# Windowed attention of a two-layer encoder: the two halves of its output added by a transfer, and part of the normalising and rounding done on GpSimd

## The chip, the cores and the metric

The kernel runs on one core of a Trainium2 chip. The core has a matrix engine (TensorE, PE in the profile), VectorE (DVE), ScalarE (ACT), GpSimd (POOL) and SyncE (SP), which only issues transfers, and 16 DMA engines. Each engine works through its own instructions in order. The metric is the device time of one execution in microseconds (us); the median over several runs is compared.

## The reference, cut to what matters

Two layers over a sequence of 1024 tokens with 1024 features. The first layer's mixer is windowed attention; the change lies in it and in the start of its output projection.

```python
def mixer_window_attn(u, mem_kv, w_in, sink, w_out, pos):
    q, k, v, xq = jnp.split(u @ w_in, [...], axis=-1)    # 16 query heads, 4 key/value heads of 64
    q = rope(q, pos); k = rope(k, pos)
    o = window_gqa_sink(q, k, v, sink)
    return jnp.concatenate([o, memory_cross_attn(xq, mem_kv)], axis=-1) @ w_out

# window_gqa_sink, per block of 128 queries, over up to 3 blocks of 128 keys:
    s = q k^T / 8, masked to |qpos - kpos| <= 128
    m = max(max_k s, sink);  p = exp(s - m)
    p = p / (sum_k p + exp(sink - m))
    o = p v
# memory_cross_attn: 4 heads of 128 over 256 memory rows, softmax, no mask
```

After the mixer come a norm, a gated feed-forward layer, and a second layer with another mixer (a gated linear recurrence). Everything is float32.

## The kernel before

Every product is made of single-pass float32r matmuls on operands that are split in two: `h` is the value rounded to float32r, `l` the remainder (`split`, line 87: ACT casts `h`, DVE subtracts to get `l`); `mm3` runs three matmuls (h·h, h·l, l·h). TensorE has therefore about three times the plain work and is the engine that all others feed.

`window()` goes through four groups `g`, one for each key/value head and its four query heads `j`. `proj(g)` makes queries, keys and values of 8 blocks of 128 tokens (`pj` banks), rotates them (DVE: two multiplications into `t1`, `t2`; POOL: the two additions into `rq`, lines 298 and 299), and TensorE turns them (`ptq`). `attend(g)` then works on 8 row blocks `n`. For each:

- scores of the four heads (`ps`, lines 374 and 375), evicted by DVE with mask and sink (line 377, `sm`), `exp` by ACT with its sum (line 381);
- the reciprocal of the sums (DVE, line 386) and the four heads' scaling by it: heads 0 and 1 on ACT (line 389), heads 2 and 3 on DVE (line 391);
- for each of up to three key blocks: four transposes of `sm` (`pt`, line 396), the split into `ph` and `pl` (lines 88 and 89), and two matmuls with `v` that add up in the bank `po` (lines 399 and 400). The stationary `v` holds the rounded part in columns 0 to 63 and the remainder in columns 64 to 127, so the rows 64 to 127 of `po` must be added to rows 0 to 63;
- that addition: ACT copies the upper rows to the tile `o` (line 402), DVE adds the lower rows (line 403).

After every second block the pair's `o` (two buffers) is sent off by SP, in two transfers: for groups 0 to 2 to the array `oT[0]` in device memory (line 414), for group 3 straight into the remainder array `ul` (line 408), where `split_moved` (lines 350 to 353) then splits it in place into `uh` and `ul`, ACT first and DVE after it.

Between the blocks of `attend` run units of cross attention (`cross_unit`; its division by the sums is line 231, one DVE instruction for four row blocks) and the projection of the next group. In group 3 there is no next group: the output projection `wo0` takes that place. `Out.begin` reads `oT[0]` back for eight token blocks (`Out.read`, ACT cast in line 466, DVE subtraction in line 467) and multiplies them by the part of the weights that belongs to the first 6 of 12 feature blocks. `Out.finish` adds the cross heads (`Out.cross`, tiles `oh`, `ol`) and the feature blocks 6 and 7, which are group 3's and come from `split_moved`.

What stands in a row on each engine is set when the program is built: the tile scheduler simulates the engines and takes instructions by priority as they become ready. `tc.issue_after(x)` keeps an instruction behind `x`. Transfers issued by SP go through a hardware queue, those issued by POOL through a software queue; only POOL's can add to what is at the target. POOL's queue also carries 24 large transfers in `window()` that add up second-layer-of-feed-forward weights (`w2s`, lines 144 and 146).

Of the kernel before, what the change touches and what calls it, by code (L numbers as in the profile page):

```python
# [8 lines left out]
F32 = mybir.dt.float32  # L9
# [4 lines left out]
ALU = mybir.AluOpType  # L14
# [35 lines left out]
def build(tc, A, out):  # L50
# [149 lines left out]
    def cross_unit(l, h, b, head, wp, tags, w0, pair, dead=False):  # L200

        wh, wl, kvh, kvl = head
        ps = tags["pj"][2].tile([P, 512], F32, tag=tags["pj"][0], bufs=tags["pj"][1], name="pj")
        for k in range(KT):
            c = slice(k * P, (k + 1) * P)
            m = slice(b * 512, (b + 1) * 512)
            mm3(ps, wh[:, c], wl[:, c], uh[:, k, m], ul[:, k, m], k == 0, k == KT - 1)
        xh, xl = pair("x", b)
        with tc.high_priority(AHEAD):
            if l == 0:  # L210
                split(xh, xl, ps)
            else:
                act.activation(xh, ps, AF.Copy, scale=XSCALE)
                dve.scalar_tensor_tensor(xl, ps, XSCALE, xh.bitcast(F32), op0=ALU.mult, op1=ALU.subtract)
        p = wp.tile([P, 4, 385 if l == 0 else 256], F32, tag="sm", bufs=tags["sm"], name="xp")[:, :, :256]
        st = {x: wp.tile([P, 4], F32, tag=x, name=x) for x in ("nm", "su", "rd")}
        for i in range(2):
            s = tags["ps"][2].tile([P, 2, 256], F32, tag=tags["ps"][0], bufs=tags["ps"][1], name="ps")
            for j in range(2):
                m = slice((2 * i + j) * P, (2 * i + j + 1) * P)  # L220
                mm3(s[:, j, :], xh[:, m], xl[:, m], kvh[:, 0, :], kvl[:, 0, :], True, True)
            e = slice(2 * i, 2 * i + 2)
            dve.reduce_max(st["nm"][:, e], s, axis=AX.X, negate=True)
            if l == 0:
                dve.tensor_tensor(st["nm"][:, e], st["nm"][:, e], xsc[:, 4 * b + 2 * i:4 * b + 2 * i + 2], op=ALU.mult)
            for j in range(2):
                q = 2 * i + j
                act.activation(p[:, q, :], s[:, j, :], AF.Exp, bias=st["nm"][:, q:q + 1],
                               scale=xsc[:, 4 * b + q:4 * b + q + 1] if l == 0 else 1.0, accum_out=st["su"][:, q:q + 1])
        dve.reciprocal(st["rd"], st["su"])  # L230
        dve.tensor_tensor(p, p, bc(st["rd"].unsqueeze(2), [P, 4, 256]), op=ALU.mult)
        po = tags["po"][b]()
        for m in range(2):
            tp = tags["pt"][2].tile([P, 4, P], F32, tag=tags["pt"][0], bufs=tags["pt"][1], name="pt")
            for q in range(4):
                pe.transpose(tp[:, q, :], p[:, q, m * P:(m + 1) * P], ident)
            ph, pl = pair("p", m)
            split(ph, pl, tp.rearrange("p a b -> p (a b)"))
            hd = slice(m * P, (m + 1) * P)
            mm3(po, kvh[:, 1, hd], kvl[:, 1, hd], ph, pl, m == 0, m == 1)  # L240
        ot = p[:, :2, :].rearrange("p a b -> p (a b)") if dead else w0.tile([P, 512], F32, tag=tags.get("xo", "xo"), bufs=1, name="xo")
        act.copy(ot, po)
        act.dma_start(oT[l][8 + h, :, b * 512:(b + 1) * 512], ot)


    def window():
# [5 lines left out]
            ap_.tile([P, 4], F32, tag=x, name=x)  # L252
        wmask = ap_.tile([P, 384], F32, bufs=1, name="wmask")
        sk = ap_.tile([P, 16], F32, bufs=1, name="sk")
        ap_.tile([64, 4, 256], F32, tag="o", bufs=2, name="o")
        for x, n in (("kh", 1), ("kl", 1), ("v", 1), ("qs", 8), ("ph", 2), ("pl", 2)):
            if x == "v":
                ap_.tile([P, NT, P], F32R, tag=x, bufs=n, name=x)
# [87 lines left out]

        marks, moved = {}, []

        def split_moved():
            ts_ = moved.pop()  # L350
            oh, ol = uh[:, 6:8, ts_], ul[:, 6:8, ts_]
            act.copy(oh, ol.bitcast(F32))
            dve.tensor_tensor(ol, ol.bitcast(F32), oh.bitcast(F32), op=ALU.subtract)

        def attend(g, qkv, blocks=range(NT)):
            qs, kh, kl, v = qkv
            for b in range(2):
                for nn in range(4):
# [1 line left out]
                    if n not in blocks:  # L360
                        continue
                    if nn % 2 == 0:
                        pairs[0] = ap_.tile([64, 4, 256], F32, tag="o", bufs=2, name="o")
                    o = pairs[0]
                    lo, hi = max(n - 1, 0), min(n + 2, NT)
                    w = (hi - lo) * P
# [13 lines left out]
                    for j in range(4):  # L380
                        marks[g, n] = act.activation(sm[:, j, :w + 1], sm[:, j, :w + 1], AF.Exp, bias=st["nm"][:, j:j + 1],
                                                     scale=-1.0, accum_out=st["su"][:, j:j + 1])
                    if moved and n % 2 == 0:
                        with tc.issue_after(marks[g, n].ins):
                            split_moved()
                    dve.reciprocal(st["rd"], st["su"])
                    for j in range(4):
                        if j < 2:
                            act.activation(sm[:, j, :w], sm[:, j, :w], AF.Copy, scale=st["rd"][:, j:j + 1])
                        else:  # L390
                            dve.tensor_scalar_mul(sm[:, j, :w], sm[:, j, :w], st["rd"][:, j:j + 1])
                    po = psp.tile([P, 4, P], F32, tag="po", bufs=1, name="po")
                    for c in range(hi - lo):
                        tp = psp.tile([P, 4, P], F32, tag="pt", bufs=2, name="pt")
# [4 lines left out]
                        pe.matmul(po, v[:, lo + c, :], ph, start=c == 0, stop=False)  # L399
                        pe.matmul(po, v[:, lo + c, :], pl, start=False, stop=c == hi - lo - 1)  # L400
                    ov = o[:, :, (nn % 2) * P:(nn % 2 + 1) * P]
                    act.copy(ov, po[64:])
                    dve.tensor_tensor(ov, po[:64], ov, op=ALU.add)
                    if nn % 2 == 1 and g == 3:
                        ts_ = slice((n - 1) * P, (n + 1) * P)
                        moved.append(ts_)
                        for hp in range(2):
                            nc.sync.dma_start(ul[hp * 64:(hp + 1) * 64, 6:8, ts_].bitcast(F32), o[:, hp::2, :])
                        if n == NT - 1:
                            split_moved()  # L410
                    elif nn % 2 == 1:
                        ts_ = slice((n - 1) * P, (n + 1) * P)
                        for hp in range(2):
                            nc.sync.dma_start(
                                oT[0][2 * g:2 * g + 2, hp * 64:(hp + 1) * 64, ts_].rearrange("a d t -> d a t"),
                                o[:, hp::2, :])
                if 4 * b + 3 not in blocks:
                    continue
                for _ in range(XU[g][b]):
# [12 lines left out]
        attend(3, cur)  # L432
        wo0.open()
        y0 = wo0.w1.tile([P, NT, 512], F32, bufs=1, name="y0")
        wo0.begin(psq, ("pj", "pj", "ptq"), [y0[:, t, :] for t in range(NT)], {6: marks[3, 2], 7: marks[3, 2]})
        psp.release()
        ap_.release()
        x0.release()
# [2 lines left out]
    class Out:  # L441
# [19 lines left out]
        def read(self, ks, c0, c1, eng, behind=None):  # L461
            c = (slice(None), slice(ks[0], ks[-1] + 1), slice(c0, c1))
            raw = ul[c].bitcast(F32)
            eng.dma_start(raw, oT[self.l][ks[0]:ks[-1] + 1, :, c0:c1].rearrange("k p t -> p k t"))
            with tc.issue_after(behind.ins) if behind else nullcontext():
                act.copy(uh[c], raw)
            dve.tensor_tensor(ul[c], raw, uh[c].bitcast(F32), op=ALU.subtract)

        def kept(self, ps, t, ks, first, last):
# [1113 lines left out]
```

## Time and profile before

| | us |
|---|---|
| median of 3 runs | 2645.28 |
| lowest, highest | 2643.67, 2646.74 |
| the profiled execution's own time | 2646.48 |
| its span, first to last instruction | 2644.4 |
| TensorE busy in the span | 2598.7 (98%) |
| DVE, ACT, POOL busy in the span | 1807.8, 1379.0, 486.7 |

`window()` takes the stretch from about 60 us to 493 us after the span's start; from 400 us on, the output projection runs between its last blocks. The profile gives a page for the whole span, and answers questions on a stretch of it: busy time of each engine by stretch, groups of equal instructions with their mean duration and what ended the idle time before them, waits by engine with what released them, and the instructions in order of time. A row such as `L403 DVE TENSOR_TENSOR o<-po,o 64x512 ... x28 | 19.0, 677` reads: line 403, on DVE, writes `o` from `po` and `o`, 64 partitions by 512 elements, 28 times, 19.0 us in all, 677 ns each.

### The profile page before, as it was taken

Reading aid. Unit: us, or ns where it says so; the run is one execution under the profiler, and the core shown is the slowest. Engines: PE = TensorE matmul, PEld = TensorE weight load, DVE = VectorE, ACT = ScalarE, POOL = GpSimd, SP = SyncE. Lnnn points to the kernel's source line nnn. Section 1 sums busy time; section 2 is a strip of 40 time slices with the busy share of each in tenths; the row PEclk is TensorE's granted clock in tenths of the full one; section 3 lists DMA queues with packets and bytes.
Section 4 is the critical chain, followed back from the end, with each engine's and each line's share of the span. In section 5 each row is a group of like instructions: output and inputs, shape, how many; then the busy total and the mean of one; then the engine's idle time right before and its main releaser. Section 6 shows DMA issues by size and latency. Waiting matters only on the chain. (4 is left out here: it accounts for less than half of the span.)

```text
span 2644.4 us, 38978 instructions
## 1 busy us (share of the span) xinstructions
PE 2598.7 (98%) x14420; PEld 2187.7 (83%) x14420; DVE 1807.8 (68%) x2875; ACT 1379.0 (52%) x2471; POOL 486.7 (18%) x552
## 2 busy tenths in 40 slices
PE   8999999999999999999999999999999999999998
PEld 8988887887888888887888888888887788888887
DVE  6778777587656565488688686887757665656447
ACT  6667767445444444455465554555534444444443
POOL 0421120221111100032234131231311111110013
PEclk9999999999999999999999999999999999999999
DMA  9782232367877757673236351103337777785666
GB/s 354 248 191 46 74 102 69 126 190 187 210 200 197 198 158 251 201 258 127 85 112 162 85 119 47 54 32 116 121 113 191 197 196 203 202 206 166 219 193 236
DMA packets 195726, 425.92 MB, mean 161 GB/s; under 512 B 20048, under 2 KB 56272, under 8 KB 189904
## 3 DMA queue, kind: packets, MB, share of 16 engines
q1 hardware_dynamic: 161552, 324.06, 38.0%
q0 software_dynamic: 24544, 90.19, 16.5%
q10 hardware_dynamic: 9440, 9.19, 1.0%
q8 instruction: 113, 1.85, 0.3%
q14 instruction: 77, 0.63, 0.1%
HBM read 330.04 MB, written 116.39 MB: 169 GB/s over the span
## 5 line engine op out<-in xcount | busy, mean ns | idle before, releaser
L89 DVE TENSOR_TENSOR wl<-st,wh 128x1024 fp32r<-128x1024 f32 (+1 forms) x238 | 262.8, 1111 | 318.0 <-ACT wh L88 291.5
L88 ACT CAST wh<-st 128x1024 fp32r<-128x1024 f32 (+1 forms) x238 | 222.1, 935 | 286.1 <-PE X L588 186.4
L83 PE MATMUL pj<-uh,wh 128*128 128x512 f32 x512 | 202.5, 396 | 3.4 <-DVE q L1139 2.0
L588 PE MATMUL X<-wl,wh 128*128 128x512 f32 x528 | 204.7, 389 | 0.3 <-DVE wl L89 0.3
L588 PE MATMUL X<-wh,wl 128*128 128x512 f32 x528 | 204.5, 389 | 0.0
L85 PE MATMUL pj<-uh,wl 128*128 128x512 f32 x512 | 202.3, 395 | 0.0
L84 PE MATMUL pj<-ul,wh 128*128 128x512 f32 x512 | 200.9, 392 | 0.1
L588 PE MATMUL X<-wh 128*128 128x512 f32 x528 | 198.7, 390 | 0.3 <-ACT c L1002 0.3
L83 PE MATMUL pj<-wh,uh 128*128 128x384 f32 (+1 forms) x512 | 189.5, 371 | 3.7 <-DVE gs L1125 2.4
L84 PE MATMUL pj<-wl,uh 128*128 128x384 f32 (+1 forms) x512 | 187.2, 366 | 0.0
L85 PE MATMUL pj<-wh,ul 128*128 128x384 f32 (+1 forms) x512 | 187.2, 366 | 0.0
L79 DVE TENSOR_TENSOR wl<-st,wh 128x1024 fp32r<-128x1024 f32 (+1 forms) x91 | 118.3, 1305 | 33.9 <-ACT wh L78 33.3
L588 PE MATMUL V<-uh,wh 128*128 128x512 f32 x336 | 130.7, 389 | 0.0
L588 PE MATMUL V<-ul,wh 128*128 128x512 f32 x336 | 130.7, 389 | 0.0
L588 PE MATMUL V<-uh,wl 128*128 128x512 f32 x336 | 130.7, 389 | 0.0
L78 ACT CAST wh<-st 128x1024 fp32r<-128x1024 f32 (+1 forms) x97 | 97.6, 1012 | 40.9 <-PE pj L84 26.9
L588 PEld LDWEIGHTS X<-wh 128*128 128x128 f32 x528 | 99.1, 188 | 21.7 <-ACT c L1002 0.7
L588 PEld LDWEIGHTS X<-wl,wh 128*128 128x128 f32 x528 | 99.1, 188 | 20.9 <-DVE wl L89 0.8
L588 PEld LDWEIGHTS X<-wh,wl 128*128 128x128 f32 x528 | 99.1, 188 | 20.7
L83 PEld LDWEIGHTS pj<-uh,wh 128*128 128x128 f32 x512 | 96.3, 188 | 22.8 <-DVE q L1139 2.9
L971 POOL TENSOR_TENSOR c<-c,g 128x512 f32<-128x512 f32 x24 | 42.6, 1793 | 388.3 <-PE X L588 160.1
L84 PEld LDWEIGHTS pj<-ul,wh 128*128 128x128 f32 x512 | 96.2, 188 | 19.2 <-DVE ul L89 0.4
(410 smaller groups left out, 7217.6 us busy)
## 6 DMA issues: line engine op xcount, KB each, us to landing
st<-hid SPq DMA_DIRECT2D x154, 256.0 KB, 3.1
st<-in_ffw_dram SPq DMA_DIRECT2D x108, 256.0 KB, 3.2
w2s<-in_ffw_dram POOLq DMA_DIRECT2D x24, 1024.0 KB, 8.5
st<-in_ffw_dram SPq DMA_DIRECT2D x46, 512.0 KB, 4.3
hid<-tt SPq DMA_DIRECT2D x88, 256.0 KB, 4.8
st<-w2s SPq DMA_DIRECT2D x88, 256.0 KB, 3.0
sx<-in_ffw_dram SPq DMA_DIRECT2D x84, 256.0 KB, 4.0
sy<-in_ffw_dram SPq DMA_DIRECT2D x42, 512.0 KB, 6.8
```

The costliest lines, as they stand in the source:

```text
L78: act.copy(h[:, :n], raw)
L79: (eng or dve).tensor_tensor(l[:, :n], raw, h[:, :n].bitcast(F32), op=ALU.subtract)
L83: pe.matmul(o, ah, bh, start=first, stop=False)
L84: pe.matmul(o, ah, bl, start=False, stop=False)
L85: return pe.matmul(o, al, bh, start=False, stop=last)
L88: act.copy(h, src)
L89: dve.tensor_tensor(l, src, h.bitcast(F32), op=ALU.subtract)
L588: last = pe.matmul(o, x, y, start=new, stop=e, skip_group_check=not first)
L971: pool.tensor_tensor(y[q][:, t, :], y[q][:, t, :], g3[:, c], op=ALU.mult)
```

## The change

1. The addition of the two halves leaves DVE. `o` gets 128 partitions, ACT copies all of `po` into it. SP sends the upper half to the target (groups 0 to 2 now in one transfer instead of two), and an adding transfer on POOL's queue (`add_parts`, line 358) puts the lower half on top. The adding transfers of a pair are issued behind the scaling of the next block that follows the pair; those of the last pair at once. `split_moved` moves from the even block after a pair to the odd one.
2. Of the four heads' scaling, head 0 stays on ACT, head 1 goes from ACT to DVE, heads 2 and 3 go from DVE to POOL.
3. In the first layer's cross units, DVE divides two of the four row blocks in one instruction, POOL the other two in two.
4. In the first layer's `Out.read`, the cast of the rows that are read back goes from ACT to POOL, and token blocks 6 and 7 no longer wait for a mark in group 3.

```diff
@@ cross_unit
         dve.reciprocal(st["rd"], st["su"])
-        dve.tensor_tensor(p, p, bc(st["rd"].unsqueeze(2), [P, 4, 256]), op=ALU.mult)
+        n = 2 if l == 0 else 4
+        dve.tensor_tensor(p[:, :n], p[:, :n], bc(st["rd"][:, :n].unsqueeze(2), [P, n, 256]), op=ALU.mult)
+        for q in range(n, 4):
+            pool.tensor_scalar_mul(p[:, q, :], p[:, q, :], st["rd"][:, q:q + 1])
@@ window
+        summed = []
+
+        def add_parts(behind=None):
+            while summed:
+                dst, src = summed.pop(0)
+                with tc.issue_after(behind.ins) if behind else nullcontext():
+                    pool.dma_start(dst, src, accum_op=ALU.add)
+
         def split_moved():
-            ts_ = moved.pop()
+            ts_ = moved.pop(0)
@@ attend
-                        pairs[0] = ap_.tile([64, 4, 256], F32, tag="o", bufs=2, name="o")
+                        pairs[0] = ap_.tile([P, 4, 256], F32, tag="o", bufs=2, name="o")
...
-                    if moved and n % 2 == 0:
+                    if moved and n % 2 == 1:
                         with tc.issue_after(marks[g, n].ins):
                             split_moved()
                     dve.reciprocal(st["rd"], st["su"])
                     for j in range(4):
-                        if j < 2:
+                        if j == 0:
                             act.activation(sm[:, j, :w], sm[:, j, :w], AF.Copy, scale=st["rd"][:, j:j + 1])
+                        elif j == 1:
+                            dve.tensor_scalar_mul(sm[:, j, :w], sm[:, j, :w], st["rd"][:, j:j + 1])
                         else:
-                            dve.tensor_scalar_mul(sm[:, j, :w], sm[:, j, :w], st["rd"][:, j:j + 1])
+                            scaled = pool.tensor_scalar_mul(sm[:, j, :w], sm[:, j, :w], st["rd"][:, j:j + 1])
+                    add_parts(scaled)
...
-                    act.copy(ov, po[64:])
-                    dve.tensor_tensor(ov, po[:64], ov, op=ALU.add)
-                    if nn % 2 == 1 and g == 3:
+                    act.copy(ov, po)
+                    if nn % 2 == 1:
                         ts_ = slice((n - 1) * P, (n + 1) * P)
-                        moved.append(ts_)
-                        for hp in range(2):
-                            nc.sync.dma_start(ul[hp * 64:(hp + 1) * 64, 6:8, ts_].bitcast(F32), o[:, hp::2, :])
+                        if g == 3:
+                            moved.append(ts_)
+                            parts = [(ul[hp * 64:(hp + 1) * 64, 6:8, ts_].bitcast(F32), slice(hp, 4, 2)) for hp in range(2)]
+                        else:
+                            rows = oT[0].rearrange("k p t -> (k p) t")[256 * g:256 * g + 256, ts_]
+                            parts = [(rows.rearrange("(j d) t -> d j t", d=64), slice(4))]
+                        for dst, js in parts:
+                            nc.sync.dma_start(dst, o[64:, js, :])
+                            summed.append((dst, o[:64, js, :]))
                         if n == NT - 1:
-                            split_moved()
-                    elif nn % 2 == 1:
...
+                            add_parts()
+                            while moved:
+                                split_moved()
...
-        wo0.begin(psq, ("pj", "pj", "ptq"), [y0[:, t, :] for t in range(NT)], {6: marks[3, 2], 7: marks[3, 2]})
+        wo0.begin(psq, ("pj", "pj", "ptq"), [y0[:, t, :] for t in range(NT)], {})
@@ Out.read
             with tc.issue_after(behind.ins) if behind else nullcontext():
-                act.copy(uh[c], raw)
+                if self.l:
+                    act.copy(uh[c], raw)
+                else:
+                    pool.tensor_copy(uh[c], raw)
```

Since the scheduler orders the program anew, the rows on every engine move. Three places matter for what follows.

POOL, in the middle of group 1. `L298`/`L299` (after the change `L301`/`L302`) are the rope additions, `L370` (`L381`) puts the sink beside the scores, `L144` is a large weight transfer. Before:

```order
L370 COPY sm<-sk 128x4
L298 TENSOR_TENSOR rq<-t_2925,t_2926 128x320
L299 TENSOR_TENSOR rq<-t_2925,t_2926 128x64
L144 DMA w2s_79<-w2s_79 32x3x2048
L370 COPY sm<-sk 128x4 x2
L298 TENSOR_TENSOR rq<-t_2960,t_2961 128x320
L299 TENSOR_TENSOR rq<-t_2960,t_2961 128x64
```

and with the change, where `L404` is the scaling of heads 2 and 3 and `L358` the adding transfer of a pair:

```order
L381 COPY sm<-sk 128x4
L404 TENSOR_SCALAR sm<-sm,rd 128x384 x4
L358 DMA oT_57<-o 64x4x256
L301 TENSOR_TENSOR rq<-t_2917,t_2918 128x320
L302 TENSOR_TENSOR rq<-t_2917,t_2918 128x64
L144 DMA w2s_79<-w2s_79 32x3x2048
L404 TENSOR_SCALAR sm<-sm,rd 128x384 x2
L381 COPY sm<-sk 128x4 x2
L301 TENSOR_TENSOR rq<-t_2952,t_2953 128x320
L302 TENSOR_TENSOR rq<-t_2952,t_2953 128x64
```

The rope additions, which waited for nothing but DVE's two multiplications, now stand behind scalings that wait for a softmax, and behind a transfer that waits for SP's.

ACT, at the end of group 3, from the copy of block 5 to the last split. `o<-po` is the copy, `uh<-ul` the split of a pair in place (lines 352, 363), `ph<-pt` the cast of a key block's transposes. Before:

```order
L402 COPY o<-po 64x4x128
L88 CAST ph<-pt 128x512
L352 CAST uh<-ul 128x2x256
L88 CAST ph<-pt 128x512 x2
L402 COPY o<-po 64x4x128
L88 CAST ph<-pt 128x512
L402 COPY o<-po 64x4x128
L352 CAST uh<-ul 128x2x256
```

with the change:

```order
L416 COPY o<-po 128x4x128
L88 CAST ph<-pt 128x512 x2
L363 CAST uh<-ul 128x2x256
L88 CAST ph<-pt 128x512
L416 COPY o<-po 128x4x128
L88 CAST ph<-pt 128x512
L416 COPY o<-po 128x4x128
L363 CAST uh<-ul 128x2x256
```

The split of pair 4-5 (the first `uh<-ul` in both) still stands two to three rows behind the copy of block 5, and the cast for block 6's third key block now stands directly behind it.

TensorE, the same place: block 6's matmuls with `v` and its neighbours. `pb<-xwh,uh` is the first product that reads the feature blocks 6 and 7 of pair 4-5. Before:

```order
L399 MATMUL po<-ph,v 128x512
L400 MATMUL po<-pl,v 128x512
L399 MATMUL po<-ph,v 128x512
L400 MATMUL po<-pl,v 128x512
L396 MATMUL pt<-ident,sm 128x128 x4
L83 MATMUL pb<-xwh,uh 128x512
L84 MATMUL pb<-xwl,uh 128x512
```

with the change:

```order
L413 MATMUL po<-ph,v 128x512
L414 MATMUL po<-pl,v 128x512
L413 MATMUL po<-ph,v 128x512
L414 MATMUL po<-pl,v 128x512
L410 MATMUL pt<-ident,sm 128x128 x4
L413 MATMUL po<-ph,v 128x512
L414 MATMUL po<-pl,v 128x512
L410 MATMUL pt<-ident,sm 128x128 x4
L83 MATMUL pb<-xwh,uh 128x512
L84 MATMUL pb<-xwl,uh 128x512
```

The third pair of `po` matmuls of block 6, which stood 11 rows behind the first product on `uh`, now stands ahead of it. From block 5's last `po` matmul up to this point TensorE has, in both programs, that matmul, eight transposes, 16 products `pb<-..,uh` of other tokens, four `po` matmuls and four transposes.

More of the change, by code (lines that the diff above doesn't have):

```diff
@@ L254, in window @@
         sk = ap_.tile([P, 16], F32, bufs=1, name="sk")
-        ap_.tile([64, 4, 256], F32, tag="o", bufs=2, name="o")
+        ap_.tile([P, 4, 256], F32, tag="o", bufs=2, name="o")
         for x, n in (("kh", 1), ("kl", 1), ("v", 1), ("qs", 8), ("ph", 2), ("pl", 2)):
@@ L401, in attend @@
                     ov = o[:, :, (nn % 2) * P:(nn % 2 + 1) * P]
-                    act.copy(ov, po[64:])
-                    dve.tensor_tensor(ov, po[:64], ov, op=ALU.add)
-                    if nn % 2 == 1 and g == 3:
+                    act.copy(ov, po)
+                    if nn % 2 == 1:
                         ts_ = slice((n - 1) * P, (n + 1) * P)
-                        moved.append(ts_)
-                        for hp in range(2):
-                            nc.sync.dma_start(ul[hp * 64:(hp + 1) * 64, 6:8, ts_].bitcast(F32), o[:, hp::2, :])
-                        if n == NT - 1:
-                            split_moved()
-                    elif nn % 2 == 1:
[L412 to L416, printed above, removed]
+                        if g == 3:
[7 more added lines that the diff above has]
+                            summed.append((dst, o[:64, js, :]))
+                        if n == NT - 1:
+                            add_parts()
+                            while moved:
+                                split_moved()
                 if 4 * b + 3 not in blocks:
```

## The prediction

> **What bounds the kernel now.** I read the page's busy shares, then busy time by stretch, then TensorE's waits in the stretches the change touches, then the groups of instructions it edits, and last the order of time at the end of group 3.
>
> ```profile
> span 2644.4 us, 38978 instructions
> PE 2598.7 (98%) x14420; PEld 2187.7 (83%) x14420; DVE 1807.8 (68%) x2875; ACT 1379.0 (52%) x2471; POOL 486.7 (18%) x552
> ```
>
> TensorE is busy 98% of the span and sets the time. No matmul is added or removed, so the change can only move TensorE's idle time and its clock. Busy time by stretch (us, counts, granted clock, share of the DMA engines):
>
> ```profile
> 60.00:150.00 90.00, 86.78 (x499) 79.75 (x497) 66.10 (x181) 55.36 (x132) 34.98 (x59) 1.00 0.78 236
> 150.00:240.00 90.00, 87.88 (x504) 79.00 (x503) 68.26 (x169) 63.46 (x156) 21.22 (x33) 0.98 0.59 134
> 240.00:345.00 105.00, 101.05 (x578) 88.53 (x578) 83.07 (x198) 77.09 (x189) 15.86 (x24) 1.00 0.21 61
> 345.00:398.00 53.00, 49.74 (x287) 45.41 (x286) 38.90 (x79) 32.30 (x72) 11.97 (x15) 0.97 0.35 105
> 398.00:458.00 60.00, 57.57 (x288) 46.85 (x287) 44.38 (x105) 47.06 (x106) 1.01 (x5) 1.00 0.24 71
> 458.00:520.00 62.00, 62.00 (x293) 51.55 (x292) 32.88 (x47) 25.46 (x54) 15.03 (x9) 1.00 0.34 107
> ```
>
> The first five rows hold 398 us, of which TensorE is busy 383.02: 15.0 us are idle. The granted clock falls to 0.98 and 0.97 in two of them, which stands for 90 x 0.02 + 53 x 0.03 = 3.4 us of full-speed work, some 1.7 in each. The last row, where the end of group 3 runs beside the output projection, has no idle at all. So at most 15.0 + 3.4 = 18.4 us can be gained, and between 458 and 520 us one can only lose. TensorE's waits from 60 to 458 us (us in total, times, longest):
>
> ```profile
> PE po L399 <- ACT ph L88: 2.8, 4, 1.1
> PE ptq L321 <- DVE kl L89: 1.9, 1, 1.9
> PE po L400 <- DVE pl L89: 1.5, 2, 1.0
> PE pt L396 <- ACT sm L389: 1.4, 2, 0.7
> PE ps L374 <- DVE nm L377: 1.3, 4, 0.4
> ...
> PE ptq L321 <- POOL rq L299: 0.9, 1, 0.9
> PE ptq L321 <- POOL rq L298: 0.8, 2, 0.5
> PE pb L83 <- ACT y L500: 0.8, 1, 0.8
> PE po L399 <- ACT xo L242: 0.7, 1, 0.7
> PE pt L396 <- DVE pl L89: 0.7, 1, 0.7
> ```
>
> They are short and spread over many producers on DVE and ACT; no one chain dominates.
>
> **The change part by part.** The edited groups from 60 to 458 us, with busy us and mean ns (the MEMSET from the whole span):
>
> ```profile
> L391 DVE TENSOR_SCALAR sm<-sm,rd 128x384 f32<-128x384 f32 x48 | 19.2, 442 | 0.4
> L403 DVE TENSOR_TENSOR o<-po,o 64x512 f32<-64x512 f32 x28 | 19.0, 677 | 7.3 <-ACT o L402 7.3
> L231 DVE TENSOR_TENSOR xp<-xp,rd 128x1024 f32<-128x1024 f32 x8 | 10.0, 1254 | 0.3
> L389 ACT ACTIVATE sm<-sm,rd 128x384 f32<-128x384 f32 x48 | 27.2, 611 | 2.3 <-DVE rd L386 2.2
> L466 ACT CAST uh<-ul 128x768 fp32r<-128x768 f32 x8 | 6.6, 835 | 4.0 <-DMA ul<-oT 4.0
> L298 POOL TENSOR_TENSOR rq<-t,t 128x320 f32<-128x320 f32 x32 | 29.0, 905 | 133.8 <-DVE t L297 75.6 <-DVE xss L1389 24.4 <-DVE rd L230 12.4
> L79 POOL TENSOR_TENSOR wl<-st,wh 128x768 fp32r<-128x768 f32 x6 | 11.2, 1880 | 2.4 <-ACT wh L78 2.4
> L1094 POOL MEMSET Az<- 128x512 f32 x2 | 1.0, 528 | 0.0
> ```
>
> *DVE and ACT get lighter.* Per block DVE drops one of two scalings (0.44) and the addition (0.68): 1.12 us; ACT drops one scaling, 0.61. Block work shortens a wait only where the late producer stands behind it, by no more than the wait's length. I take each wait down by what its engine saves: the four on `ph` by 0.61 each, 2.4 together; the one on `kl` by 1.1; the two on `pl` (line 400) whole, 1.5; the four on `nm` whole, 1.3; `y` 0.6; `xo` 0.6; `pl` (line 396) 0.7. That is -8.2 us. If stalls of this sort are what brings the clock down, one of the two drops goes: -1.7. The rest of the 15 us idle has no recorded releaser; I take nothing from it. Between nothing and the 15.0 + 3.4 lies -9.9.
>
> *Scaling on POOL.* No row shows POOL scaling by a column. Below stands the memset, 528 x 384/512 = 0.40 us for 384 elements; above, half of line 79 (two operands, twice the width), 0.94. I take the middle, 0.67, since the scaling reads one full operand, the memset none and line 79 two. A block's pair takes 1.34. POOL and DVE can also keep each other out:
>
> ```profile
> 92.79 3.65 POOL L79 TENSOR_TENSOR wl<-st,wh 128x768 fp32r<-128x768 f32 x2
> 92.95 3.90 DVE L391 TENSOR_SCALAR sm<-sm,rd 128x256 f32<-128x256 f32 x2
> ```
>
> Two DVE scalings took 3.90 us for well under 0.9 while POOL ran. The trace therefore shows one of the two held up until the other engine is done; in a block DVE now scales (0.44) at the same moment as POOL, so POOL's pair ends after up to 1.34 + 0.44 = 1.78, where ACT's pair ended after 2 x 0.61 = 1.22. The two waits of `pt` on ACT's scaling become waits on POOL's, 0.56 longer each: +1.1. The Trainium skill, page "GPSIMD Engine Reference", section "1. Specifications", says that GpSimd shares its SBUF interface with VectorE, which speaks against giving the two engines work at one moment; by it, every block would pay in one order or the other; the row above agrees, with 3.90 us.
>
> *The rope additions* now stand on POOL behind scalings. The three recorded waits on `rq` (1.7 us) each grow by up to one scaling, 0.67: +2.0. Behind the same scalings stand the adding transfers and the large weight transfers of lines 144 and 146; the first of these are read after group 2's attention, the second in the second layer, so their 0.6 to 1.1 us of issue is costed at nothing. With 85 of 398 us POOL was idle enough; its new work is 28 pairs x 1.34 + 8 reads + divisions + 12 issues, about 77 us, 41% in all.
>
> *Taken at nothing.* The read casts: 8 x 0.835 leave ACT and come to POOL at 0.79 to 1.88 (the same two bounds); no wait of TensorE is on `uh` from line 466. The cross division: DVE's 1254 halves, POOL takes two scalings of 256; the wait on `xo` lies behind it and is counted. ACT's copy keeps 512 elements per partition on twice the partitions. SP issues 12 transfers fewer in groups 0 to 2. `o` has two buffers and is free only when the adding transfer has read it; the order leaves over a block (398/28 = 14 us) for that. The cover for all of these is other blocks' and units' products in TensorE's order; without it, a late `o` would hold ACT's copy and the `ph` cast behind it.
>
> *End of group 3.* Here something new enters a chain that TensorE waits on. Before, for pair 4-5 (start, us busy):
>
> ```profile
> 477.00 0.39 PE L400 MATMUL po<-pl,v 128*128 128x512 f32 x1
> 477.43 0.58 ACT L402 COPY o<-po 64x512 f32<-64x512 f32 x1
> 478.05 0.68 DVE L403 TENSOR_TENSOR o<-po,o 64x512 f32<-64x512 f32 x1
> 478.76 1.25 SPq L408 DMA_DIRECT2D ul<-o  x2
> 481.86 0.62 ACT L352 CAST uh<-ul 128x512 fp32r<-128x512 f32 x1 [3.23 <-DMA ul<-o]
> 483.01 0.47 PE L83 MATMUL pb<-xwh,uh 128*128 128x512 f32 x1
> ```
>
> The cast waited 3.23 us for the transfer and began 4.9 us after the last `po` matmul; TensorE got to its first product on `uh` 6.0 us after that matmul, in time. With the change the chain drops the addition (0.7), so the upper half is in place at 4.9 - 0.7 = 4.2 us; then POOL issues the adding transfer. Rows for that, median us from issue to landing in the last column:
>
> ```profile
> ul<-o SPq DMA_DIRECT2D x8, 128.0 KB, 2.4
> sy<-sx POOLq DMA_DIRECT2D x42, 256.0 KB, 4.2
> ```
>
> `sy<-sx` is the same kind, an adding transfer between tiles, with twice the bytes; the plain `ul<-o` has the right size. I take 4.2 as the nearer kind and 2.4 as the lower bound; the second half's issue runs beside the first half's flight. The cast starts at 8.4, ends at 9.0. The cast of block 6's third key block (0.58, as the copy) now stands directly behind it, so `ph` comes at about 9.6, plus some 0.3 us of handing over between five engines (an estimate; the gaps in the rows are 0.03 to 0.04, a transfer's end is not among them): 9.9. TensorE has between the two `po` matmuls the same instructions as it had before its first product on `uh`, so it waits 9.9 - 6.0 = 3.9 us (2.1 with the lower bound), and one clock drop of 1.7 with it: +5.6. Pair 2-3 has more room, at most 0.7, left to the range; of pair 6-7 the order leaves 48 products ahead of the use, 48 x 62/293 = 10.2 us, against the 9.0 of the cast's end: nothing.
>
> The page "DMA: Bandwidth & Descriptors" of the Trainium skill, section "Anatomy of one DMA — SWDGE (gpsimd) path", fits a transfer from that queue as a fixed 2.0 us plus its bytes at 436 GB/s: an estimate of 2.3 us for 128 KB, by which the stall would be 2.0 instead of 3.9. For 256 KB the same fit gives 2.6 where the row above has 4.2, so this trace does not bear the fit out for adding transfers.
>
> *Sum.* -9.9 + 1.1 + 2.0 + 5.6 = -1.2 us against the profiled execution, 2646.5: 2645.3. That execution is 1.2 above the median of the runs, so against the median the forecast is 2644.1.
>
> **The rivals.** A measurement of this kernel tells about 0.2% (5.3 us) from no change.
>
> *The end costs nothing.* If the adding transfer lands as soon as a plain one and the casts stay ahead of TensorE, only -9.9 + 3.1 = -6.8 is left: 2638.5. For it: the lower bound takes away 1.8 of the 3.9. Against: the chain is serial, 4.2 us before the transfer even begins, and TensorE has 6.0.
>
> *GpSimd becomes the late one (slower).* One mechanism: the scaling takes the upper bound, 0.94, and is held up by DVE. Then a pair takes 2 x 0.94 + 0.44 = 2.3 us against ACT's 1.22, +1.1 at every place where scaled scores come just in time. Waits on scores and casts make 9 to 12 such places, +10 to +13, with the clock drops of two of them (3.4): about +13 in place of the 1.1 and 2.0. -9.9 + 5.6 + 13 = +9: 2654. It decides from about 1 us per scaling. For it: line 79's 1880 and the 3.90 above. Against: the transposes come many products after the scaling in TensorE's order.
>
> *The waits don't go.* If the waits come from the order and another producer is late right behind the one that was sped up, the -9.9 shrinks to nothing while the end stays: +5.6, 2651. For it: the 15 us are spread over the many kinds of waits listed above, none longer than 1.9.
>
> **How the numbers follow.** Gain and end cost about equal: 0.45, 2644. End free: 0.30, 2638.5, faster. GpSimd late: 0.17, 2654, slower. Waits stay: 0.08, 2651, slower. Hence faster 0.30, same 0.45, slower 0.25. The range runs from the second case with a little more of the 18.4 us gained, 2635, to just short of the third, 2653. The likeliest case alone reaches from 2640 to 2649.
>
> **What would show it.** DVE busy from 60 to 458 us down by some 40 us from 300.7, ACT by some 25, POOL from 85 to about 160; line 404's mean near 0.67 us; TensorE's idle there from 15 to about 9. Near 480 to 490 us: the cast in line 363 waiting over 6 us for the adding transfer, `po` waiting on `ph` for some 4 us, a slice of lower clock. I am wrong if line 404 is 1 us or more and the waits name POOL, if the adding transfer is there in 2.4 us, or if the waits on `ph`, `pl` and `nm` are as many as before.

## The result, and the profile after

The changed kernel took 2662.0 us (median of 6 runs, 2659.5 to 2668.3) against 2646.0 for the kernel before beside it: ratio 1.0065, 95% interval 1.0051 to 1.0080. It is 16 us slower. The forecast was 2644.1, range 2635 to 2653: wrong in size and in sign. Of the executions in this document two, 3058.7 us of the new scaling alone and 5560.2 us of the kernel without SP's four loads, ran in a slow state of the chip and are left out of the medians.

The profiled execution of the changed kernel is one of its faster ones, with a span of 2657.7 us, 13.3 more than before. The page's first lines, and busy time by stretch as in the prediction (PE, PEld, DVE, ACT, POOL, granted clock, DMA share, GB/s):

```profile
span 2657.7 us, 39000 instructions
PE 2602.2 (98%) x14420; PEld 2187.4 (82%) x14420; DVE 1779.2 (67%) x2811; ACT 1355.4 (51%) x2431; POOL 603.6 (23%) x660
```

```profile
60.00:150.00 90.00, 87.05 (x491) 80.14 (x490) 60.09 (x166) 49.61 (x121) 52.54 (x72) 0.98 0.81 237
150.00:240.00 90.00, 84.53 (x483) 75.30 (x482) 62.71 (x152) 59.28 (x147) 47.94 (x54) 0.98 0.69 144
...
458.00:520.00 62.00, 56.08 (x258) 45.40 (x258) 28.25 (x41) 24.79 (x53) 20.32 (x16) 0.97 0.45 111
```

From 60 to 458 us ACT lost 26 us of work, as forecast (some 25), DVE 28 where some 40 was forecast, and POOL went from 85 to 195 us, not to 160. TensorE's idle time there did not fall from 15.0 to about 9; it rose to 17.0. TensorE's share of 98% says nothing; the stretches do. From 458 to 520 us it was never idle before; now it idles 5.9 us and the clock falls to 0.97. From 150 to 240 us it is busy 84.5 instead of 87.9. Comparing the start of the same matmuls in both traces, TensorE runs behind the kernel before by up to 6 us near 170 us, by 2.2 at 450 us, and by 10.9 from 520 us on.

TensorE's waits, from 60 to 458 us and (second fence) from 455 to 525 us:

```profile
PE pt L410 <- POOL sm L404: 3.5, 3, 2.3
PE po L413 <- ACT ph L88: 3.4, 2, 2.9
PE ps L385 <- DVE nm L388: 2.8, 5, 1.6
PE ptq L324 <- POOL rq L301: 2.5, 2, 1.6
```

```profile
PE pb L83 <- ACT uh L363: 4.5, 2, 2.7
PE pb L84 <- DVE xwl L79: 1.3, 1, 1.3
```

A wait on POOL's scaling is new, and the end of group 3 has two waits on the split of a pair, not one, and a third on the remainder of a weight (`xwl`, at 519 us). On POOL itself, from 60 to 458 us, the scaling costs:

```profile
L404 POOL TENSOR_SCALAR sm<-sm,rd 128x384 f32<-128x384 f32 x48 | 66.3, 1424 | 59.8 <-DVE rd L397 58.8 <-DVE nm L225 1.0
L234 POOL TENSOR_SCALAR xp<-xp,rd 128x256 f32<-128x256 f32 x16 | 18.1, 1162 | 12.4 <-DVE rd L230 9.9 <-PE pj L83 2.4
```

That is 1.42 us where the forecast took 0.67 and had 0.94 as its upper end. It looks like the culprit. The experiments say otherwise.

The end of group 3 in order of time, pair 4-5 and then pair 6-7:

```profile
479.25 0.39 PE L414 MATMUL po<-pl,v 128*128 128x512 f32 x1
479.68 0.59 ACT L416 COPY o<-po 128x512 f32<-128x512 f32 x1 [0.18 <-PE po L414]
...
483.23 1.99 POOL L358 DMA_DIRECT2D ul<-o  x2 [9.59 <-DMA ul<-o]
...
487.88 0.62 ACT L363 CAST uh<-ul 128x512 fp32r<-128x512 f32 x1 [2.84 <-DMA ul<-o]
...
488.55 0.50 PE L83 MATMUL pb<-xwh,uh 128*128 128x512 f32 x1 [1.79 <-ACT uh L363]
...
490.16 0.63 PE L83 MATMUL pb<-xwh,uh 128*128 128x512 f32 x1
490.59 0.63 PE L84 MATMUL pb<-xwl,uh 128*128 128x512 f32 x1
...
497.64 1.92 POOL L358 DMA_DIRECT2D ul<-o  x2 [12.42 <-DMA ul<-o]
...
507.04 0.62 ACT L363 CAST uh<-ul 128x512 fp32r<-128x512 f32 x1 [12.34 <-DMA ul<-o]
...
507.71 0.50 PE L83 MATMUL pb<-xwh,uh 128*128 128x512 f32 x1 [2.75 <-ACT uh L363]
```

For pair 4-5 the chain runs as forecast: copy, SP's half, adding transfer, cast; the cast ends 9.25 us after the last `po` matmul began, where 9.0 was worked out. TensorE waits 1.8 us, and behind that eight matmuls start 0.43 us apart instead of 0.23: the clock drop, 1.6 us (granted clock 0.50 from 490 to 492 us). For pair 6-7 the cast begins only 9.4 us after POOL issued the adding transfers, instead of 4.65, and TensorE waits another 2.75; no slower matmuls follow this one (granted clock 1.00 from 506 to 510 us).

### The profile page after: what moved, and what is told of

Same layout as the page of the kernel before. It is cut to its first block, busy times and chain, and to the rows that moved or that the text cites. A ratio compares the mean times of both kernels' runs of the same rounds, so it can differ in the third digit from the quotient of the medians.

```text
span 2657.7 us, 39000 instructions
## 1 busy us (share of the span) xinstructions
PE 2602.2 (98%) x14420; PEld 2187.4 (82%) x14420; DVE 1779.2 (67%) x2811; ACT 1355.4 (51%) x2431; POOL 603.6 (23%) x660
## 5 line engine op out<-in xcount | busy, mean ns | idle before, releaser
L1255 POOL TENSOR_TENSOR E<-EP,q 128x256 f32<-128x256 f32 x64 | 52.5, 820 | 284.8 <-DVE EP L1248 247.1
L606 PEld LDWEIGHTS X<-wl,wh 128*128 128x128 f32 x528 | 99.1, 188 | 21.3 <-DVE wl L89 0.8
```

The costliest lines, as they stand in the source:

```text
L606: last = pe.matmul(o, x, y, start=new, stop=e, skip_group_check=not first)
L1255: pool.tensor_tensor(gl, pl_, ql, op=ALU.mult)
```

## The experiments

All were timed against the kernel before, run beside them; what is compared below is mostly one variant with another, each by its median. The kernel before took 2644.6 to 2645.3 us beside them. A ratio's interval is about 0.1% to either side, some 2.5 us, so a difference of two variants under about 3.5 us is not clear of noise.

**Without adding transfers.** The changed kernel with the whole of part 1 taken back: the addition on DVE, `o` on 64 partitions, SP's two transfers for each pair, the split in its old place. The lines of the addition:

```diff
-                    act.copy(ov, po)
+                    act.copy(ov, po[64:])
+                    dve.tensor_tensor(ov, po[:64], ov, op=ALU.add)
```

> Two theories of the changed kernel's loss. A, the adding transfers: they lengthen the end of group 3 by some 8.7 us (the lag of TensorE behind the kernel before grows from 2.2 to 10.9 us between 480 and 520 us) and stand at the head of GpSimd's queue with scalings behind them. B, the scaling on GpSimd: 1.24 us at the least and 1.42 in the mean for 384 elements, where 0.67 was forecast, eats what DVE and ACT save. This kernel is the changed one with the addition of the halves back on DVE and no adding transfers. A: at least the 8.7 of the end and 2 to 6 us in the window come back, about 2646 to 2649 if before is 2646 and after 2661. B: only the end comes back, 2652, and TensorE still waits on POOL's scaling.

2636.45 us, ratio 0.9971 (0.9959 to 0.9982): 8.2 us faster than before, and faster than either kernel. What costs is what theory A named, and it costs far more than A said.

**Scaling as before, the rest changed.**

```diff
-                        if j == 0:
+                        if j < 2:
                             act.activation(sm[:, j, :w], sm[:, j, :w], AF.Copy, scale=st["rd"][:, j:j + 1])
-                        elif j == 1:
-                            dve.tensor_scalar_mul(...)
                         else:
-                            scaled = pool.tensor_scalar_mul(...)
+                            scaled = dve.tensor_scalar_mul(...)
```

> The changed kernel with the four heads' scaling as it was before (two on ACT, two on DVE); adding transfers, split division and GpSimd read casts stay. A (adding transfers): the end keeps its 8.7 us and the window stays within 3 us of the kernel before, 2655 to 2658. B (scaling): the window gets faster than before by the saving of the additions, 2 to 6 us, so 2649 to 2653; no wait of TensorE on POOL's scaling is left in either case.

2654.1 us, ratio 1.0037 (1.0024 to 1.0050). In size that lies between the two theories. By the start of the same matmuls TensorE runs some 10 us behind the kernel before from 160 to 310 us; at 440 us the two are level, since the kernel before has a wait of its own near 390 us. TensorE's longest waits here are on the rope additions and on the scores.

```profile
PE ptq L324 <- POOL rq L301: 7.6, 4, 5.5
PE ps L385 <- DVE nm L388: 5.6, 4, 4.4
```

**Each part alone, on the kernel before.** Adding transfers alone:

> The kernel before with only the adding transfers (part 1). A: 2646 plus the end's 8.7 plus what they cost in the window, 2655 to 2660. B: 2646 plus 8.7 less 2 to 5 us for the 0.68 us that DVE saves per block, 2650 to 2653. If the sum of this and of the scaling alone falls short of the whole loss, the two make it worse together (a scaling that waits on POOL behind an adding transfer).

2665.0 us, ratio 1.0086 (1.0072 to 1.0100), above what either theory said and no better than the whole change. The order of time on POOL, and then TensorE's, shows one place: POOL stood idle 14 us ahead of an adding transfer, with the rope additions behind it, and TensorE waited 7.6 us for them.

```profile
155.18 1.01 POOL L355 DMA_DIRECT2D oT<-o  x1 [13.98 <-DMA oT<-o]
155.83 1.24 POOL L298 TENSOR_TENSOR rq<-t,t 128x320 f32<-128x320 f32 x1
```

```profile
157.12 0.48 PE L321 MATMUL ptq<-ident,rq 128*128 128x128 f32 x1 [7.62 <-POOL rq L298]
```

The new scaling alone:

> The kernel before with only the new scaling (part 2: head 0 on ACT, 1 on DVE, 2 and 3 on GpSimd). A: within 3 us of the kernel before, or faster by up to 5. B: slower by 4 to 9 us, with TensorE waits on POOL's scaling of 3 us or more in all.

2640.6 us, ratio 0.9985 (0.9976 to 0.9994), 4.0 us faster. Theory B falls: with POOL's scaling at 1418 ns here too, the kernel does not get slower when nothing holds POOL's queue up.

**Where the adding transfers cost.** In groups 0 to 2 alone; in group 3 alone; in groups 1 and 2 alone. In each, the other groups add on DVE, as in the first experiment (with group 3, its split goes back to its old place too), and all else is the changed kernel. The lines of the addition:

```diff
-                    act.copy(ov, po)
+                    if g == 3:          # second kernel: if g < 3; third: if g in (0, 3)
+                        act.copy(ov[64:], po[64:])
+                        dve.tensor_tensor(ov[64:], po[:64], ov[64:], op=ALU.add)
+                    else:
+                        act.copy(ov, po)
```

> The adding transfers cost some 25 us against the changed kernel without them (2636 against 2662). Two places are proposed. A1, groups 0 to 2: an adding transfer waits at the head of GpSimd's queue for SP's transfer of the other half, and rope additions and scalings stand behind it (in the kernel with the adding transfers alone GpSimd stood idle 13.98 us ahead of one). A2, the end: the adding transfers of group 3's last two pairs. This is the changed kernel with the addition of group 3 alone back on DVE. If A1 carries the mid part: TensorE is some 10 us later at 440 us than without adding transfers and the end adds nothing, 2646 to 2651. If the end were the whole, 2636 to 2640.

> The changed kernel with adding transfers in group 3 alone, the addition on DVE in groups 0 to 2. A2 gives 2636 plus about 8.7 (two waits on the cast of line 363 of 1.8 and 2.7 us, and a clock drop of about 1.7 to 3.4), 2643 to 2648. If only the middle mattered, 2636 to 2640.

> Adding transfers in groups 1 and 2 alone; groups 0 and 3 add on DVE. A1 places the loss where the large weight transfers of lines 144 and 146 share the DMA engines (60 to 240 us), where SP's half took 11.8 to 15.0 us to land instead of 3.1. Then most of the mid loss is gone, 2636 to 2642. If an adding transfer costs its wait anywhere, about two thirds of the mid loss stays, 2643 to 2648.

2653.4 us (ratio 1.0034, 1.0022 to 1.0045), 2645.1 (0.9997, 0.9988 to 1.0006) and 2643.7 (0.9993, 0.9985 to 1.0002). Against the kernel without adding transfers, groups 0 to 2 cost 16.9 us and group 3 costs 8.6; together 25.5, which is what lies between 2636.5 and 2662.0. Of the 16.9, groups 1 and 2 make 7.2 and group 0 the rest, 9.7. The first is above its expectation (2646 to 2651), the second within it. The third came out as "an adding transfer costs its wait anywhere": the stretch with the large weights holds most of the loss, not all of it.

**Is it the wait?** The order of time on POOL and TensorE, in the kernel with adding transfers in groups 0 to 2:

```profile
147.29 1.18 POOL L144 DMA_DIRECT2D w2s<-in_ffw_dram  x1
160.46 1.05 POOL L358 DMA_DIRECT2D oT<-o  x1 [11.99 <-DMA oT<-o]
161.17 4.63 POOL L404 TENSOR_SCALAR sm<-sm,rd 128x384 f32<-128x384 f32 x4
```

```profile
162.86 0.48 PE L410 MATMUL pt<-ident,sm 128*128 128x128 f32 x1 [5.95 <-POOL sm L404]
```

The adding transfer heads POOL's queue and waits 12 us for SP's transfer of the other half; four scalings, whose reciprocals DVE had done at 148.7 and 154.1 us, stand behind it, and TensorE waits 5.95 us. By the start of the same matmuls TensorE is 2 us behind the kernel without adding transfers at 153 us and 9 to 10 from 156 us on: close to half of the 16.9 is lost at this one place. The next kernel keeps the adding transfers, their size and their places in POOL's queue, but they add the finished sum into another array, so that they do not wait for SP:

```diff
-                    act.copy(ov, po)
+                    act.copy(ov[64:], po[64:])
+                    dve.tensor_tensor(ov[64:], po[:64], ov[64:], op=ALU.add)
...
-                        parts = [(rows.rearrange("(j d) t -> d j t", d=64), slice(4))]
...
-                        for dst, js in parts:
-                            nc.sync.dma_start(dst, o[64:, js, :])
-                            summed.append((dst, o[:64, js, :]))
+                        rows = [... for x in oT]
+                        nc.sync.dma_start(rows[0], o[64:])
+                        summed.append((rows[1], o[64:]))
```

> In groups 0 to 2 DVE adds the halves as before, and GpSimd besides issues the same twelve adding transfers from `o`, at the same places of its queue and of the same size, but into rows of the second layer's array, which are written over later: they wait for DVE and for their queue, not for SP's transfer, and no read waits for them. Group 3 adds on DVE. If the wait for the other half at the head of GpSimd's queue (and the read-back's wait for the sum) makes the 17 us that adding transfers cost in groups 0 to 2, this is near the kernel without them, 2636 to 2641. If the issue, the traffic or the buffer that is held makes them, it stays at 2649 to 2654.

2637.5 us, ratio 0.9968 (0.9955 to 0.9980): 1.1 above the kernel without adding transfers. Of 16.9 us, 15.8 go with the waiting; neither the issue, the traffic nor the buffer makes them. Here no read-back waits for an adding transfer either, so the 15.8 hold both waits, POOL's and the read-back's. At the same place:

```profile
147.30 1.66 POOL L358 DMA_DIRECT2D oT<-o  x1
148.74 2.73 POOL L404 TENSOR_SCALAR sm<-sm,rd 128x384 f32<-128x384 f32 x2
```

The Trainium skill, page "DMA: Bandwidth & Descriptors", section "Anatomy of one DMA — SWDGE (gpsimd) path", says that the DMA engines don't wait on semaphores, and that any wait on a semaphore happens on the issuing sequencer before dispatch. The 11.99 us above agree: the wait belongs to POOL, and everything in its queue shares it.

**Why is SP's half late?** Two kernels without the 24 weight transfers of lines 144 and 146 in the first layer, one with adding transfers in groups 0 to 2, one without any. Their first feed-forward part reads plain weights of the same size in place of the sums that are left out:

```diff
             ins = yield
+            if l == 0:
+                continue
             with tc.issue_after(ins.ins):
```

> The kernel with adding transfers in groups 0 to 2 (group 3 on DVE), without the 24 weight transfers of lines 144 and 146 in the first layer, whose sums are left out. To be read against the next kernel, which leaves the same out and adds on DVE. If SP's half is late because it shares the DMA engines with those weights, the two differ by 4 to 8 us instead of 17, and no wait of GpSimd ahead of an adding transfer exceeds 5 us. If not, they still differ by 14 us or more.

> The kernel without adding transfers, and without the same 24 weight transfers: the reference for the one before. The weights hold nothing up here by either theory, 2632 to 2638 (2636.5 with them).

2641.7 us (ratio 0.9985, 0.9976 to 0.9994) and 2643.7 (0.9993, 0.9984 to 1.0002): without the weight transfers the kernel with adding transfers is not the slower one, where 4 to 8 us were expected; GpSimd's longest wait for SP's half is 4.8 us, within the 5 expected. Time from issue to landing for the transfers of `o` (min, median, max), with the weights and then without:

```profile
DMA to landing us min/median/max: 2.3/3.4/15.5
```

```profile
DMA to landing us min/median/max: 2.3/3.1/6.1
```

The stretch from 150 to 240 us of the same two kernels shows TensorE busy 81.06 us at 0.96 with them, 88.44 at 1.00 without:

```profile
150.00:240.00 90.00, 81.06 (x457) 71.79 (x456) 59.22 (x142) 54.94 (x135) 46.63 (x53) 0.96 0.66 140
```

```profile
150.00:240.00 90.00, 88.44 (x525) 79.36 (x524) 64.72 (x166) 62.56 (x157) 43.37 (x52) 1.00 0.25 58
```

The weights alone do not hold TensorE back there; the kernel with them and without adding transfers has:

```profile
150.00:240.00 90.00, 87.75 (x522) 79.00 (x520) 67.70 (x172) 63.64 (x155) 44.86 (x53) 1.00 0.56 127
```

The reference without adding transfers missed its expectation: 2643.7, where 2632 to 2638 was expected. From 230 to 370 us it runs some 2 to 3 us ahead of the kernel with the weights. It then loses some 7 us at one place, where group 3's transposes wait for the rope additions and the granted clock is 0.94 (345 to 398 us):

```profile
PE ptq L326 <- POOL rq L304: 3.7, 1, 3.7
```

The kernel before has its own long wait at that place (`kl`, 1.9 us, and the 0.97 of 345 to 398 us). Each edit reorders the program, and this place makes or breaks several us. So the difference of the two, -2.0, carries no sign; the stretches do. By the start of the same matmuls the kernel with adding transfers is some 2 us behind its reference at 370 us without the weights, and 13.6 with them.

**One head on POOL instead of two**, without adding transfers:

```diff
-                        if j == 0:
+                        if j < 2:
...
-                        elif j == 1:
+                        elif j == 2:
```

> The kernel without adding transfers, with one head's scaling on GpSimd instead of two (heads 0 and 1 on ACT, 2 on DVE, 3 on GpSimd). If GpSimd's 1.24 to 1.42 us per scaling lie on the path, this gains up to 3 us, 2633 to 2636. If they are covered, ACT's 0.61 us more per block costs 0 to 3 us, 2636 to 2640.

2639.8 us, ratio 0.9981 (0.9972 to 0.9990): 3.4 more than with two heads there, which noise could make; a gain, which a scaling on the path was to bring, it is not. How much of the 3.4 is the reordering just named was not separated.

**Parts 3 and 4 alone.** The kernel before with half the cross division and the read casts on GpSimd:

> The kernel before with parts 3 and 4 alone: half the cross division and the read casts on GpSimd. From the difference of the kernel without adding transfers (2636.5) and the scaling alone (2641.2): 4.7 us faster than before, about 2640, if the parts add up; the forecast took them at nothing, 2643 to 2647.

2641.5 us, ratio 0.9986 (0.9977 to 0.9994): 3.3 us faster, where the forecast had nothing. With the 4.0 of the scaling it makes 7.3 of the 8.2 us that parts 2 to 4 gain together.

**The end of group 3.** On the kernel with adding transfers in group 3 alone: SP's four loads behind the last pair replaced, and the last pair back on DVE:

```diff
-                g1 = grow(wp, A["norm_g"][l, 1:2, :], "g1")
...
+                    for x in (g1, g2, *xs.values()):
+                        pool.memset(x, 1.0)
```

> The kernel with adding transfers in group 3 alone (2645.1), without the four loads that SP issues right behind the last pair (two rows of norm weights spread over 128 partitions, two token blocks of the input): GpSimd fills these tiles with ones instead, so the scale and the residual of two blocks are left out. If the loads slow the last adding transfers, these land in about 4 us instead of 8, the second wait on the cast of line 363 (2.7 to 2.9 us) and its clock drop go, 2639 to 2642. If the landing comes from something else, 8 us and the wait stay, 2644 to 2646.

```diff
-                    if g == 3:
+                    if g == 3 and n < NT - 2:
                         act.copy(ov, po)
```

> The same kernel, with the loads, but with the last pair's (6-7) addition on DVE; pair 4-5 and 2-3 keep their adding transfers. If the end is two waits of 1.8 and 2.7 us with a clock drop of 1.7 to 2 us each, 4 to 5 of its 8.6 us go, 2640 to 2642. If the chain of pair 4-5, which the forecast had at 5.6, is most of it, 2642 to 2645.

2641.1 us (ratio 0.9988, 0.9979 to 0.9997), within its expectation, and 2638.1 (0.9973, 0.9962 to 0.9983), below both of its own, against 2645.1. Order of time with the loads, then without: POOL's adding transfers of the last pair and ACT's cast:

```profile
487.09 1.92 POOL L358 DMA_DIRECT2D ul<-o  x2 [12.74 <-DMA ul<-o]
...
496.29 0.62 ACT L363 CAST uh<-ul 128x512 fp32r<-128x512 f32 x1 [12.45 <-DMA ul<-o]
```

```profile
485.67 1.92 POOL L358 DMA_DIRECT2D ul<-o  x2 [11.19 <-DMA ul<-o]
...
490.29 0.62 ACT L363 CAST uh<-ul 128x512 fp32r<-128x512 f32 x1 [7.88 <-DMA ul<-o]
```

Without the loads the cast follows 4.6 us after the issue instead of 9.2, and the second wait is gone; that is worth 4.0 us. Taking the last pair's adding transfers away altogether is worth 7.0 of the 8.6. The wait of pair 4-5 stays in both (1.8 and 1.9 us) and leaves 1.7 us by the medians, which is not clear of noise. The 3.0 us between the two kernels do not show in the kept traces, which are level at 540 us; the second one's is the slowest of its eight executions (2641.1).

The clock drop does not come with every such wait. In the kernel without the loads TensorE waits as long as it did in the changed kernel, and the clock stays up:

```profile
477.82 0.51 PE L83 MATMUL pb<-xwh,uh 128*128 128x512 f32 x1 [1.76 <-ACT uh L363]
```

```profile
478.00:480.00 2.00, 2.00 (x9) 1.61 (x10) 1.79 (x4) 1.22 (x3) 0.00 (x0) 1.00 0.00 0
```

## Why the prediction was wrong

*What bounds the kernel, and where time could be gained* held. Parts 2 to 4 gain 8.2 us of the 18.4 that TensorE had idle or slowed. Without adding transfers its idle time from 60 to 458 us falls from 15.0 to 10.7, and the granted clock is 1.00 in all five stretches.

*DVE and ACT get lighter, -9.9.* The size came out near by luck. The 8.2 come without DVE's saving of the addition, 3.3 of them from the steps that were "taken at nothing", and they are 4.3 us of idle time and both clock drops (3.4), where 8.2 of waits and one drop (1.7) were worked out. Waits on `nm`, taken whole, are still there (2.2 us, six times).

*Scaling on POOL, 0.67 us.* Wrong by a factor of two and outside its bounds: 1.42 in the mean, 1.24 at the least. The row for it was already quoted: line 298, 905 ns for 320 elements, makes 905 x 384/320 = 1.09. A memset and half of a wider instruction were the farther rows. The Trainium skill, page "GPSIMD Engine Reference", section "3.1 Elementwise — side-by-side cycle accounting", has 4497 ns for an addition of 2048 elements, by which 384 would take 0.84, an estimate; the measured 1.24 is above it. The error did no harm that shows: the scaling alone still makes the kernel faster.

*The adding transfers of groups 0 to 2, "costed at nothing".* This is the step that failed. The prediction priced their issue (0.6 to 1.1 us) and looked at the buffer they hold, not at the wait that each brings to the head of POOL's queue. The order of POOL's rows had shown what stands behind them (rope additions, scalings) and what they wait for; the wait was given no length. Beside the large weight transfers SP's half took 11.8 us in the changed kernel and up to 15.5 in the others. The trace of the kernel before had it, behind a median that hides it: of its transfers of `o`, the two issued at 140.8 and 141.4 us landed 10.8 and 12.0 us later.

```profile
DMA to landing us min/median/max: 2.3/2.4/12.0
```

Measured: 16.9 us. (The sums of the weight transfers, which the prediction has read in the second layer, are read in the first layer's feed-forward part, from 1003 us on; nothing hangs on it here.)

*The end of group 3, +5.6.* The mechanism was right, the sum near (8.6), the split wrong. Pair 4-5 was to cost 5.6; it cost 3.4 in the changed kernel's trace (a wait of 1.8 and a clock drop of 1.6) and about 1.7 by the medians, where the drop does not come every time: the cast that stands behind the split belongs to block 7's first key block, not to block 6's third as the account of the order had it, so TensorE waited on `uh` alone, and reached it 7.5 us after the last `po` matmul instead of 6.0. Pair 6-7 was taken at nothing on a landing of 4.2 us. It landed in over 8 beside SP's next loads, and cost 7.0 by the medians, of which the kept traces show 4.5.

*The rivals.* "GpSimd becomes the late one" had the sign, the engine and 2654, the nearest of the four. Its mechanism was not the one: not the scaling's price at 9 to 12 places, but a few long waits of the whole queue (14.0 us where the adding transfers stand alone, 12.0 in groups 0 to 2, 8.3 in the changed kernel). The prediction's own signs of being wrong came in part: line 404 took over 1 us with 3.5 us of waits that name POOL, and waits on `nm` and `pl` were no fewer than before.

Not settled is the share, within groups 1 and 2's 7.2 us, of a second path: the read-back of `oT[0]` on SP waits for the adding transfers, and the load of the next cross head's keys stands behind it on SP. In that kernel ACT waited 2.47 us for this load and TensorE 2.0 for the cast behind it. SP's read-backs waited 21.3 us in all for transfers of `o` there, against 5.4 in the kernel without adding transfers. No kernel took that path apart.

## What to carry to other kernels

An adding transfer that needs another transfer to have landed puts that landing time on the engine that issues it; price it by the slowest landing beside the heaviest traffic at that place, not by the median, and count everything queued behind. Do the addition on an engine instead: here 0.68 us of DVE per block was cheaper than twenty transfers. An expensive instruction on an idle engine can be free while a cheap one that waits is not.

## What the runs showed of the hardware

- A plain transfer of 256 KB, 3.1 us without the weight transfers, landed 15.5 us after its issue at 144.2 us, beside four adding transfers that were in flight one after another (two of 1 MB, two of 768 KB; the last landed at 160.3 us).
- An adding transfer of 128 KB landed in about 4 us alone and in over 8 beside four loads of SP's.
- GpSimd's scaling of 128 rows by a column takes 1.24 us for 384 elements at the least and 1.42 in the mean; DVE's took 0.44 in the mean before and 0.46 to 0.52 where GpSimd scales two of the other heads.
- After a wait of TensorE of 1.8 us eight matmuls ran at half the rate (starts 0.43 us apart instead of 0.23, granted clock 0.50) in the changed kernel; after one of 1.76 us in another kernel, and one of 2.75 in the changed one, none did.
